# First block of a fused encoder layer: x and V weights fetched and split in parts, seven still matmuls for ten

## The chip, the cores and the metric

The kernel runs on one core of a Trainium2 chip. The core has a matrix engine (TensorE, PE in the profile, with its weight loads as PEld), VectorE (DVE), ScalarE (ACT), GpSimd (POOL) and SyncE (SP). SP, ACT and POOL can issue DMAs; their issues are listed as SPq, ACTq and POOLq. The metric is the device time of one execution in microseconds; less is better.

## The reference

One layer of a hybrid encoder over 512 tokens of width 1024, in float32. Only its opening matters here: a normalised x times a wide input projection.

```python
h = rms_norm(x, g_mix_pre[l])
proj = h @ w_in[l]
q_f, k_f, v_f, f_logit, q_c, k_c, v_c = jnp.split(proj, splits, axis=-1)
```

Columns 1024 to 1535 of `w_in` give the V of the first attention group, and columns 1536 to 1543 its eight forget-gate logits. Two kinds of attention, an output projection, cross-attention into 256 memory tokens and a SwiGLU layer follow.

## The kernel before

x is read transposed, so that its 1024 features lie on the partitions in eight blocks of 128 (`xt`, index k) and its 512 tokens run along the row. The weights come by the same blocks of 128 rows. Every float32 operand is split in two: a high part in a rounded format that the matrix engine takes at its faster rate, and a low part, which is the value less its high part. A product is three matmuls (`mm3`, lines 142 to 146): high by high, high by low, low by high.

The row factor of the RMS norm is applied after the projection, and the gain before it. So x can be multiplied as soon as a block has landed. `x_block` (L293) makes the high part `hTh` of one block on ScalarE (L294) and the low part `hTl` on VectorE (L295). It scales by the gains, which lie in the tile `gn` and come with a DMA on ScalarE's queue (L234).

The first projection is that of V and the gates, 520 columns, cut in `halves` (L279): columns 256 to 519 first (264 wide), then 0 to 255. `load_v` (L246) fetches the 520 columns of a block in one DMA on SyncE's queue (L248) into a tile `raw` with three buffers; `load_x` (L243) fetches x (L244). `v_weights` (L281) makes the high parts `vhi`, for block 0 on VectorE (L285) and for others on ScalarE (L287), and then the low parts `vlo` on VectorE (L289). `v_products` (L307) takes four groups of 128 tokens by two halves by three matmuls, 24 in all, for one block, and adds them up in six accumulators over the eight blocks.

The loads are issued in the order x block 0, V block 0, x block 1, V block 1, x blocks 2 and 3, and so on in pairs (L318 to L328). Beside these, ScalarE squares x in pairs of blocks (`squares`, L301) and VectorE adds the squares (`add_squares`, L305, L338) for the row factor, which a matmul with a column of ones sums up (L255) and a matmul with the identity spreads (L264).

Ahead of the first product the matrix engine runs ten "still" matmuls of a zeroed 128x128 float32 tile with itself (L240, L241), whose result is not used. ScalarE makes one small activation, `warm` (L236), ahead of which its function table is loaded.

The order of the instructions on each engine is fixed when the program is built: a scheduler places them by its own estimate of when their operands are there, with the order of the text as priority. Memsets of later stages (L400, L401), for one, stand on VectorE ahead of block 0.

Of the kernel before, what the change touches and what calls it, by code (L numbers as in the profile page):

```python
# [8 lines left out]
F32 = mybir.dt.float32  # L9
F32R = mybir.dt.float32r  # L10
AF = mybir.ActivationFunctionType
ALU = mybir.AluOpType
AX = mybir.AxisListType

P = 128
SEQ = 512
# [12 lines left out]
G_MIX, G_MEMQ, G_MEMKV, G_FFN, G_FOX, G_CHK, B_F = 0, 8, 16, 24, 32, 36, 40  # L29
# [7 lines left out]
def hybrid_block_kernel(  # L37
# [19 lines left out]
    nc = tc.nc  # L57
    act, dve, pool, pe = nc.scalar, nc.vector, nc.gpsimd, nc.tensor

    cst = ctx.enter_context(tc.tile_pool(name="cst", bufs=1))  # L60
    wp = ctx.enter_context(tc.tile_pool(name="wp", bufs=2))
# [9 lines left out]
    def f32(ap):  # L71
        return ap.bitcast(F32)
# [15 lines left out]
    def gcol(c):  # L88
        return gn[:, c : c + 1]

    def small(n, name):
        serial[0] += 1
        return cst.tile([P, n], F32, tag="small" if n <= NT else "wide", name=f"{name}{serial[0]}", bufs=24 if n <= NT else 4)
# [132 lines left out]
    hTh = big.tile([P, KB, SEQ], F32R, tag="sA", name="hTh")  # L226
    hTl = big.tile([P, KB, SEQ], F32R, tag="sB", name="hTl")
# [3 lines left out]
    with tc.tile_pool(name="mix", bufs=1, reuse_waits="tile") as bp:  # L231
        xt = ox.tile([P, KB, SEQ], F32, tag="x1", name="xt")
        xs = ox.tile([P, KB, SEQ], F32, tag="x2", name="xs")
        nc.scalar.dma_start(gn, gains)  # L234
        warm = small(1, "warm")
        act.activation(warm, ones, AF.Square)  # L236
        acc0 = [bank(tag) for tag in ("s", "s", "a", "o")]
        acc1 = [bank("a"), bank("a")]
        warmed = bank("t")
        for j in range(10):  # L240
            pe.matmul(warmed[:, :P], still, still, start=True, stop=True)  # L241

        def load_x(k, n):  # L243
            nc.sync.dma_start(xt[:, k : k + n, :], x_t[k * P : (k + n) * P, :].rearrange("(k p) n -> p k n", p=P))  # L244

        def load_v(k, n):  # L246
            raw = wp.tile([P, n, 520], F32, tag="raw", name=f"rawv{k}", bufs=3)
            nc.sync.dma_start(raw, w_in[k * P : (k + n) * P, 1024:1544].rearrange("(k p) n -> p k n", p=P))  # L248
            return raw
# [26 lines left out]
        def at_block(parts, k, n=1):  # L276
            each = KB // len(parts)
            return parts[k // each][:, k % each : k % each + n, :]
        halves = (slice(256, 520), slice(0, 256))  # L279

        def v_weights(raw, k, n):  # L281
            for j, cs in enumerate(halves):
                h = at_block(vhi[j], k, n)
# [6 lines left out]
                    out=at_block(vlo[j], k, n), in0=raw[:, :, cs], in1=f32(at_block(vhi[j], k, n)), op=ALU.subtract  # L290
                )

        def x_block(k):  # L293
            act.activation(hTh[:, k, :], xt[:, k, :], AF.Copy, scale=gcol(G_MIX + k))  # L294
            dve.scalar_tensor_tensor(  # L295
                out=hTl[:, k, :], in0=xt[:, k, :], scalar=gcol(G_MIX + k), in1=f32(hTh[:, k, :]),
                op0=ALU.mult, op1=ALU.subtract,
            )

        def squares(k):  # L300
            act.activation(xs[:, k : k + 2, :], xt[:, k : k + 2, :], AF.Square, scale=1.0 / 32.0)  # L301
# [13 lines left out]
                    at_block(vhi[1], k)[:, 0, :], at_block(vlo[1], k)[:, 0, :], k == 0 and t % 2 == 0, k == KB - 1 and t % 2 == 1,  # L315
                )

        load_x(0, 1)  # L318
        raws = {0: load_v(0, 1)}
        load_x(1, 1)  # L320
        raws[1] = load_v(1, 1)
        load_x(2, 2)
# [3 lines left out]
        for k, n in ((0, 1), (1, 1), (2, 2), (4, 2), (6, 2)):  # L326
            if k not in raws:
                raws[k] = load_v(k, n)  # L328
            for j in range(k, k + n):
                x_block(j)  # L330
            v_weights(raws[k], k, n)
            if k:
                squares(k if k > 1 else 0)
            if k in (2, 6):
                add_squares(k - 2, k)
            if k == 6:
                add_squares(0, 4)
                dve.tensor_tensor(out=xs[:, 0, :], in0=xs[:, 0, :], in1=xs[:, 1, :], op=ALU.add)  # L338
            for j in range(k, k + n):
                v_products(j)  # L340
                if j == 6:
                    rcol = feature_rstd(xs, range(1), NT, "rx")
        act.copy(rrow, spread(rcol, NT))

        def v_tile(name):
            return bp.tile([P, NT, 4, 128], F32R, tag="V", name=f"V{name}", bufs=2)

        def raw_v(v, t, a, r):
            a4 = a.rearrange("p (h d) -> p h d", h=4)
            act.activation(v[:, t, :, 0:64], a4, AF.Copy, scale=r)  # L350
            dve.scalar_tensor_tensor(
                out=v[:, t, :, 64:128], in0=a4, scalar=r, in1=f32(v[:, t, :, 0:64]),
                op0=ALU.mult, op1=ALU.subtract,
            )

        z = cst.tile([P, NT, 8], F32, tag="z", name="z")
        first_v = [v_tile("01"), v_tile("00")]
        for t in range(NT):
            r = rcol[:, t : t + 1]
            raw_v(first_v[0], t, acc0[t][:, :256], r)  # L360
            dve.scalar_tensor_tensor(
                out=z[:, t, :], in0=acc0[t][:, 256:264], scalar=r, in1=gn[:, B_F : B_F + 8],
                op0=ALU.mult, op1=ALU.add,
            )
        for t in range(NT):
            raw_v(first_v[1], t, acc1[t // 2][:, (t % 2) * 256 : (t % 2 + 1) * 256], rcol[:, t : t + 1])

        pts = []
        for b in range(2):
# [33 lines left out]

        def group_proj(name):
            q, kt, kl = [], [], []
            if first_v:
                v = first_v.pop(0)
            else:
                v = v_tile(name)
                hi, lo = unit()  # L410
                for t in range(NT):
                    ts = slice(t * P, (t + 1) * P)
                    if t % 2 == 0:
                        acc = bank("a")
                    a = acc[:, (t % 2) * 256 : (t % 2 + 1) * 256]
                    for k in range(KB):
                        mm3(a, hTh[:, k, ts], hTl[:, k, ts], hi[:, k, :], lo[:, k, :], k == 0, k == KB - 1)
                    raw_v(v, t, a, rcol[:, t : t + 1])

            def fin_q(b, acc):  # L420
                t = bp.tile([P, 2, SEQ], F32R, tag="Q", name=f"Q{name}{b}", bufs=3)
                for h, own, other in ((0, H0, H1), (1, H1, H0)):
                    act.activation(t[own, h, :], acc[own, :], AF.Copy, scale=0.125)
                    dve.scalar_tensor_tensor(
                        out=t[other, h, :],
                        in0=acc[own, :],
                        scalar=0.125,
                        in1=f32(t[own, h, :]),
                        op0=ALU.mult,
                        op1=ALU.subtract,  # L430
                    )
                q.append(t)

            def fin_k(b, acc):
                t = bp.tile([P, 2, SEQ], F32R, tag="T", name=f"T{name}{b}", bufs=3)
                l = klz[nkl[0] % len(klz)]
                nkl[0] += 1
                for h, own, other in ((0, H0, H1), (1, H1, H0)):
                    act.copy(t[own, h, :], acc[own, :])
                    dve.tensor_tensor(  # L440
                        out=l[own, h, :], in0=acc[own, :], in1=f32(t[own, h, :]), op=ALU.subtract
                    )
                    act.copy(t[other, h, :], acc[own, :])
                kt.append(t)
                kl.append(l)

            proj_blocks(fin_q)
            proj_blocks(fin_k)
            return q, kt, kl, v
# [158 lines left out]
        for n, (side, g) in enumerate(order):  # L608
            with later(-20):
                q, kt, kl, v = group_proj(f"{side}{g}")  # L610
# [51 lines left out]
    with tc.tile_pool(name="cross", bufs=1, reuse_waits="tile") as cp:  # L662
# [20 lines left out]
        with later(-115):  # L683
            for c in range(4):
                hi, lo = unit()
                acc = bank("a")
                for b in range(2):
                    for k in range(KB):
                        cs = slice(b * P, (b + 1) * P)
# [7 lines left out]
                    out=kT[:, 1, 2 * c : 2 * c + 2, :], in0=a3,  # L697
                    in1=f32(kT[:, 0, 2 * c : 2 * c + 2, :]), op=ALU.subtract,
# [7 lines left out]
        for half in range(2):  # L706
            hi, lo = unit()
            for t in range(NT):
                acc = bank("a")
                for k in range(4):  # L710
                    ts = slice(t * P, (t + 1) * P)
                    mm3(acc, oh[:, 4 + k, ts], ol[:, 4 + k, ts], hi[:, k, :], lo[:, k, :], k == 0, k == 3)
                cs = slice(half * 512, (half + 1) * 512)
                m = mix[:, t, cs]
                dve.scalar_tensor_tensor(
                    out=m, in0=acc, scalar=rs_g[1][:, t : t + 1], in1=m, op0=ALU.mult, op1=ALU.add
# [3 lines left out]
                if half:  # L720
                    r = small(1, "prs")
                    dve.scalar_tensor_tensor(
                        out=r, in0=mix_ms[:, 0, t : t + 1], scalar=EPS, in1=mix_ms[:, 1, t : t + 1],
                        op0=ALU.add, op1=ALU.add,
# [3 lines left out]
                        out=mix[:, t, :], in0=mix[:, t, :], scalar=r, in1=xo[t], op0=ALU.mult, op1=ALU.add  # L728
# [15 lines left out]
        for half in range(2):  # L744
# [12 lines left out]
            cs = slice(half * 512, (half + 1) * 512)  # L757
# [6 lines left out]
        for h in range(4):  # L764
            for o in (oTh, oTl):
                t = quarter("oT").rearrange("p (k n) -> p k n", k=2)
                o += [t[:, 0], t[:, 1]]
        for h in range(4):
            hi, lo = unit()
            q = qq[:, h % 2]  # L770
            for b in range(2):
                acc = bank("a")
                cs = slice(b * P, (b + 1) * P)
                for k in range(KB):
# [3 lines left out]
                    out=q[:, 1, b, :], in0=acc, scalar=1.0 / 16.0, in1=f32(q[:, 0, b, :]),  # L778
                    op0=ALU.mult, op1=ALU.subtract,
                )  # L780
            p = cp.tile([P, NT, NMEM], F32, tag="xp", name=f"xp{h}", bufs=2)
            for i in range(0, NT, 2):
                s = bank("s")
                for j in range(2):
# [8 lines left out]
                    out=nm, in_=s.rearrange("p (j n) -> p j n", j=2), axis=AX.X, op=ALU.max, negate=True  # L793
# [9 lines left out]
                for j in range(2):  # L803
                    dve.tensor_scalar(
                        out=p[:, i + j, :], in0=p[:, i + j, :], scalar1=rs[:, j : j + 1],
# [8 lines left out]
                cs = slice(i * P, (i + 2) * P)  # L814
# [79 lines left out]
        raws, places = [0], []  # L894
# [629 lines left out]
```

## Time and profile before

| | |
|---|---|
| median of 3 runs | 769.16 us (768.88 to 769.38) |
| the profiled execution | 769.24 us |
| its span, first to last instruction | 767.5 us |
| mean granted TensorE clock | 0.997 |
| DMA, bytes moved over the span | 80.05 MB, mean 104 GB/s |
| issues of `xt`, block 0 and 1 | 2, of 256 KB |
| issues of `rawv`, block 0 and 1 | 2, of 260 KB |
| issue of `gn` | 24 KB, 2.9 us to landing |

A row of the timeline gives the start in us from the first instruction, the length in us, the engine, the line of the kernel, the operation, output <- inputs, shapes and a count. In brackets stands the idle time of the engine before it and what ended it. Rows that follow one another on an engine and are alike are merged; their lengths overlap, since engines are pipelined. A float32 still matmul leaves two records. In a table of windows a row holds the window, its length, the busy time of the engine asked for (with its instructions), the granted clock, the DMA engines' busy share and GB/s. In a list of DMA issues the last number is the time from issue to landing.

### The profile page before, as it was taken

What the parts mean: (1) busy time and instruction counts of PE and PEld (TensorE: products, weight loads), DVE (VectorE), ACT (ScalarE), POOL (GpSimd) and SP (SyncE); (2) the same over time, 40 slices, a digit from 0 to 9 for tenths busy, and PEclk for the clock granted to TensorE, in tenths of its full rate; (3) what the DMA queues carried; (4) which work ended last, traced back from release to release, by engine and by line L of the source; (5) the groups of instructions that cost most, each with busy time, mean ns of one, the idle gap of its engine ahead of it and who ended that gap; (6) DMA issues with size and microseconds to landing.
All of it is one profiled execution on the core that took longest, in us unless ns stands there. A gap on an engine that the chain in (4) does not pass through costs nothing.

```text
span 767.5 us, 12862 instructions
## 1 busy us (share of the span) xinstructions
PE 752.7 (98%) x4988; PEld 674.4 (88%) x4988; DVE 595.7 (78%) x1083; ACT 442.9 (58%) x811; POOL 63.6 (8%) x105
## 2 busy tenths in 40 slices
PE   9999999999999999999999999999999999999996
PEld 9977888887778988877778899999999999898985
DVE  8667889789886688555653897999999999987746
ACT  7558889667875457444563635555555557543411
POOL 1001132100321201000001200000000000000001
PEclk9999999999999999999999999999999999999998
DMA  7522123422323735421341132333333323233312
GB/s 268 145 64 76 29 56 95 126 83 60 109 80 83 265 120 186 118 76 59 108 147 48 56 102 65 110 111 110 111 111 110 111 84 110 83 115 107 108 58 109
DMA packets 60748, 80.05 MB, mean 104 GB/s; under 512 B 2704, under 2 KB 43664, under 8 KB 60688
## 3 DMA queue, kind: packets, MB, share of 16 engines
q1 hardware_dynamic: 59264, 74.49, 30.9%
q0 software_dynamic: 1280, 4.72, 1.8%
q8 instruction: 39, 0.64, 0.4%
q14 instruction: 21, 0.17, 0.1%
q10 hardware_dynamic: 144, 0.02, 0.0%
HBM read 77.13 MB, written 2.10 MB: 103 GB/s over the span
## 4 chain that ended last, share of the span: by engine, by line
PE 87%; ACT 6%; DVE 4%; issue 2%; POOL 1%; DMA 1%; DVEq 0%; POOLq 0%; ACTq 0%
PE ps_a L144 13%; PE ps_a L146 13%; PE ps_a L143 13%; PE ps_t L1130 3%; PE ps_t L1127 3%; PE ps_s L1128 3%; PE ps_t L1128 3%; PE ps_s L1127 3%; PE ps_s L1130 3%; PE ps_s L143 2%; PE ps_s L146 2%; PE ps_s L144 2%; PE ps_t L552 2%; PE ps_o L561 2%; PE ps_s L533 1%
## 5 line engine op out<-in xcount | busy, mean ns | idle before, releaser
L126 DVE TENSOR_TENSOR lo<-raw,hi 128x1024 fp32r<-128x1024 f32 x56 | 68.2, 1223 | 20.6 <-ACT hi L125 20.4
L146 PE MATMUL ps_a<-hTh,lo 128*128 128x512 f32 x192 | 76.7, 399 | 0.0
L144 PE MATMUL ps_a<-hTl,hi 128*128 128x512 f32 x192 | 75.9, 395 | 0.0
L143 PE MATMUL ps_a<-hTh,hi 128*128 128x512 f32 x192 | 75.9, 395 | 0.0
L125 ACT CAST hi<-raw 128x1024 fp32r<-128x1024 f32 x56 | 57.8, 1047 | 25.5 <-PE ps_a L144 21.2
L923 DVE TENSOR_TENSOR ring_lo<-sums,ring_hi 128x1024 fp32r<-128x1024 f32 (+1 forms) x39 | 46.7, 1196 | 12.9 <-ACT ring_hi L922 8.5
L922 ACT CAST ring_hi<-sums 128x1024 fp32r<-128x1024 f32 (+1 forms) x39 | 40.1, 1029 | 17.2 <-PE ps_s L1128 15.6
L922 ACT CAST ring_hi<-fraw 128x1024 fp32r<-128x1024 f32 (+1 forms) x26 | 26.7, 1033 | 33.5 <-DVE fraw L1009 13.9
L923 DVE TENSOR_TENSOR ring_lo<-fraw,ring_hi 128x1024 fp32r<-128x1024 f32 (+1 forms) x26 | 31.0, 1201 | 14.2 <-ACT ring_hi L922 14.0
L144 PEld LDWEIGHTS ps_a<-hTl,hi 128*128 128x128 f32 x192 | 36.1, 188 | 6.4
L146 PEld LDWEIGHTS ps_a<-hTh,lo 128*128 128x128 f32 x192 | 36.1, 188 | 6.4
L143 PEld LDWEIGHTS ps_a<-hTh,hi 128*128 128x128 f32 x192 | 36.2, 188 | 5.6
L547 ACT ACTIVATE p<-p,nm 128x128 f32<-128x128 f32 (+1 forms) x64 | 36.1, 565 | 8.1 <-DVE nm L537 7.2
L554 ACT CAST pth<-ps_t 128x128 fp32r<-128x128 f32 (+1 forms) x64 | 27.0, 424 | 14.5 <-PE ps_t L552 13.7
L555 DVE TENSOR_TENSOR ptl<-ps_t,pth 128x128 fp32r<-128x128 f32 (+1 forms) x64 | 30.7, 487 | 5.0 <-ACT pth L554 3.7
L552 PE MATMUL ps_t<-ident,p 128*128 128x128 f32 x160 | 28.2, 275 | 1.1 <-DVE p L549 0.8
L549 DVE TENSOR_SCALAR p<-p,rc 128x128 f32<-128x128 f32 (+1 forms) x64 | 26.8, 418 | 0.1
L552 PEld LDWEIGHTS ps_t<-ident,p 128*128 128x128 f32 x160 | 19.3, 140 | 7.3 <-issue 2.4
L143 PE MATMUL ps_a<-hi,oh 128*128 128x512 f32 x64 | 25.5, 399 | 0.0
L1130 PE MATMUL ps_a<-b,ring_lo 128*128 128x256 f32 (+1 forms) x93 | 25.5, 276 | 0.0
L1127 PE MATMUL ps_a<-b,ring_hi 128*128 128x256 f32 x92 | 25.5, 277 | 0.0
L1128 PE MATMUL ps_a<-b,ring_hi 128*128 128x256 f32 x92 | 25.4, 276 | 0.0
(546 smaller groups left out, 2760.9 us busy)
## 6 DMA issues: line engine op xcount, KB each, us to landing
raw<-in_dram SPq DMA_DIRECT2D x64, 512.0 KB, 3.9
fraw<-in_dram SPq DMA_DIRECT2D x26, 512.0 KB, 3.5
place<-in_dram SPq DMA_DIRECT2D x21, 512.0 KB, 4.3
more_room<-in_dram SPq DMA_DIRECT2D x15, 512.0 KB, 4.3
cb<-in_dram SPq DMA_DIRECT2D x8, 256.0 KB, 2.7
xo<-in_dram POOLq DMA_DIRECT2D x4, 512.0 KB, 7.6
out_dram<-yd SPq DMA_DIRECT2D x8, 256.0 KB, 2.0
rawv<-in_dram SPq DMA_DIRECT2D x3, 520.0 KB, 6.3
```

The source lines that it names most:

```text
L125: act.copy(hi[:, j : j + n, :], raw)
L126: dve.tensor_tensor(out=lo[:, j : j + n, :], in0=raw, in1=f32(hi[:, j : j + n, :]), op=ALU.subtract)
L143: pe.matmul(dst, sh, mh, start=first, stop=False)
L144: pe.matmul(dst, sh, ml, start=False, stop=False)
L146: pe.matmul(dst[:, to], sl, mh[:, to], start=False, stop=last)
L547: act.activation(p[:, :n], p[:, :n], AF.Exp, bias=nm, scale=-1.0, accum_out=sm)
L552: pe.transpose(tp[:, k * P : (k + 1) * P], p[:, k * P : (k + 1) * P], ident)
L922: act.copy(h2, v)
L923: dve.tensor_tensor(out=l2, in0=v, in1=f32(h2), op=ALU.subtract)
L1127: pe.matmul(dst, w[0][:, k, :], b[:, 0, k, :], start=first and k == 0, stop=False, skip_group_check=more)
L1128: pe.matmul(dst, w[0][:, k, :], b[:, 1, k, :], start=False, stop=False, skip_group_check=more)
L1130: pe.matmul(dst[:, to], w[1][:, k, :], b[:, 0, k, to], start=False, stop=last and k == 3, skip_group_check=more,)
```

## The change

Block 0 of x is fetched in two DMAs, tokens 0 to 255 and tokens 256 to 511, both on SyncE's queue. The first is written at the head of the stage, the second where the whole load stood. The V weights of block 0 are fetched in two DMAs by the column halves: columns 256 to 519 on ScalarE's queue behind the gains, columns 0 to 255 on SyncE's queue behind the second half of x. For block 0, `x_block` makes the high part in two activations of 256 tokens and the low part in two VectorE instructions. The still matmuls are seven. A list is renamed from `first_v` to `ready_v`, since `first_v` is now a function; the rename changes nothing else.

```diff
+        raws = {0: wp.tile([P, 1, 520], F32, tag="raw", name="rawv0", bufs=3)}
+        token_halves = (slice(0, 256), slice(256, 512))
+        halves = (slice(256, 520), slice(0, 256))
+
+        def first_x(to):
+            nc.sync.dma_start(xt[:, 0, to], x_t[0:P, to])
+
+        def first_v(queue, cs):
+            queue.dma_start(raws[0][:, 0, cs], w_in[0:P, 1024 + cs.start : 1024 + cs.stop])
+
+        first_x(token_halves[0])
         nc.scalar.dma_start(gn, gains)
+        first_v(nc.scalar, halves[0])
         warm = small(1, "warm")
...
-        for j in range(10):
+        for j in range(7):
             pe.matmul(warmed[:, :P], still, still, start=True, stop=True)
...
-        def x_block(k):
-            act.activation(hTh[:, k, :], xt[:, k, :], AF.Copy, scale=gcol(G_MIX + k))
-            dve.scalar_tensor_tensor(
-                out=hTl[:, k, :], in0=xt[:, k, :], scalar=gcol(G_MIX + k), in1=f32(hTh[:, k, :]),
-                op0=ALU.mult, op1=ALU.subtract,
-            )
+        def x_block(k, parts=(slice(0, SEQ),)):
+            for to in parts:
+                act.activation(hTh[:, k, to], xt[:, k, to], AF.Copy, scale=gcol(G_MIX + k))
+            for to in parts:
+                dve.scalar_tensor_tensor(
+                    out=hTl[:, k, to], in0=xt[:, k, to], scalar=gcol(G_MIX + k), in1=f32(hTh[:, k, to]),
+                    op0=ALU.mult, op1=ALU.subtract,
+                )
...
-        load_x(0, 1)
-        raws = {0: load_v(0, 1)}
+        first_x(token_halves[1])
+        first_v(nc.sync, halves[1])
         load_x(1, 1)
         raws[1] = load_v(1, 1)
...
             for j in range(k, k + n):
-                x_block(j)
+                x_block(j, token_halves if j == 0 else (slice(0, SEQ),))
             v_weights(raws[k], k, n)
```

More of the change, by code (lines that the diff above doesn't have):

```diff
@@ L278, in at_block @@
             return parts[k // each][:, k % each : k % each + n, :]
-        halves = (slice(256, 520), slice(0, 256))
         def v_weights(raw, k, n):
@@ L356, in hybrid_block_kernel @@
         z = cst.tile([P, NT, 8], F32, tag="z", name="z")
-        first_v = [v_tile("01"), v_tile("00")]
+        ready_v = [v_tile("01"), v_tile("00")]
         for t in range(NT):
             r = rcol[:, t : t + 1]
-            raw_v(first_v[0], t, acc0[t][:, :256], r)
+            raw_v(ready_v[0], t, acc0[t][:, :256], r)
             dve.scalar_tensor_tensor(
@@ L365, in hybrid_block_kernel @@
         for t in range(NT):
-            raw_v(first_v[1], t, acc1[t // 2][:, (t % 2) * 256 : (t % 2 + 1) * 256], rcol[:, t : t + 1])
+            raw_v(ready_v[1], t, acc1[t // 2][:, (t % 2) * 256 : (t % 2 + 1) * 256], rcol[:, t : t + 1])
         pts = []
@@ L405, in group_proj @@
             q, kt, kl = [], [], []
-            if first_v:
-                v = first_v.pop(0)
+            if ready_v:
+                v = ready_v.pop(0)
             else:
```

## The prediction

> **What bounds the kernel now.** I read the page first: its head, the busy shares and the chain that ended last.
>
> ```profile
> span 767.5 us, 12862 instructions
> PE 752.7 (98%) x4988; PEld 674.4 (88%) x4988; DVE 595.7 (78%) x1083; ACT 442.9 (58%) x811; POOL 63.6 (8%) x105
> PE 87%; ACT 6%; DVE 4%; issue 2%; POOL 1%; DMA 1%; DVEq 0%; POOLq 0%; ACTq 0%
> ```
>
> TensorE (PE) has work in flight for 752.7 of 767.5 us and holds 87% of the chain. So what the change can win is PE time at the very start, and only as far as PE is not starved later instead. The profiled execution took 769.24 us, 1.74 above its span and 0.08 above the median of the runs shown (769.16).
>
> Next I read the start in order of time, engine by engine (start, length, engine, line, output<-inputs).
>
> ```profile
> 1.05 4.37 PE L241 MATMUL ps_t<-rrow 128*128 128x128 f32 x20 [1.05 <-DVE ones L80]
> 5.55 0.48 PE L143 MATMUL ps_s<-vhi,hTh 128*128 128x264 f32 x2
> ...
> 8.51 0.29 PE L143 MATMUL ps_s<-vhi,hTh 128*128 128x264 f32 x1
> ...
> 6.00:8.00 2.00, 2.00 (x19) 1.00 1.02 383
> ...
> 20.00:30.00 10.00, 10.00 (x86) 1.00 0.59 159
> ```
>
> The still matmuls fill PE to 5.42 (1.05 + 4.37), the first product starts at 5.55, and from 6 to 30 us PE is busy all of every window (the first and the last of five stand here: length, PE busy, clock, DMA share, GB/s). One block of x costs 24 products: 8.51 − 5.55 = 2.96 us, 0.123 each. A first product that starts earlier therefore moves everything behind it, unless operands come too late.
>
> Where do the first operands come from? These are ScalarE (ACT) and VectorE (DVE), with the three ACT instructions ahead of them.
>
> ```profile
> 0.73 0.40 ACTq L234 DMA_DIRECT2D gn<-in_dram  x1
> 1.16 1.28 ACT L236 ACT_TABLE_LOAD   x1 [1.16 <-PEq L1511]
> 2.46 0.20 ACT L236 ACTIVATE warm<-ones 128x1 f32<-128x1 f32 x1
> 3.69 0.72 ACT L294 ACTIVATE hTh<-xt,gn 128x512 fp32r<-128x512 f32 x1 [1.03 <-DMA gn<-in_dram]
> 5.27 0.72 ACT L294 ACTIVATE hTh<-xt,gn 128x512 fp32r<-128x512 f32 x1 [0.86 <-DMA xt<-in_dram]
> 4.44 0.75 DVE L295 SCALAR_TENSOR_TENSOR hTl<-xt,gn,hTh 128x512 fp32r<-128x512 f32 x1 [0.88 <-ACT hTh L294]
> 5.11 0.49 DVE L285 CAST vhi<-rawv 128x264 fp32r<-128x264 f32 x2
> 5.52 0.77 DVE L289 TENSOR_TENSOR vlo<-rawv,vhi 128x264 fp32r<-128x264 f32 x2
> ```
>
> ACT makes x's high part at 3.69, when the gains have landed. DVE then makes the low part, and only behind it, at 5.11, casts the first V weights. That cast ends at 5.40 and the stills at 5.42, so **two things end together** ahead of 5.55: the stills and the cast. Removing one alone wins almost nothing; the change takes up both.
>
> **The change part by part.** Prices of half pieces, from groups by shape in the first 16 us, and landings of the first transfers, one DMA view each:
>
> ```profile
> L289 DVE TENSOR_TENSOR vlo<-rawv,vhi 128x264 fp32r<-128x264 f32 x2 | 0.9, 430 | 0.3 <-ACT vhi L287 0.3
> L289 DVE TENSOR_TENSOR vlo<-rawv,vhi 128x256 fp32r<-128x256 f32 x2 | 0.8, 420 | 0.0
> L285 DVE CAST vhi<-rawv 128x264 fp32r<-128x264 f32 x1 | 0.3, 291 | 0.0
> L287 ACT CAST vhi<-rawv 128x256 fp32r<-128x256 f32 x1 | 0.4, 406 | 0.0
> ...
> xt<-in_dram SPq DMA_DIRECT2D x1, 256.0 KB, 2.7
> gn<-in_dram ACTq DMA_DIRECT2D x1, 24.0 KB, 2.9
> ...
> rawv<-in_dram SPq DMA_DIRECT2D x1, 260.0 KB, 3.2
> 1.18 0.42 SPq L248 DMA_DIRECT2D rawv<-in_dram  x1
> 1.64 0.42 SPq L244 DMA_DIRECT2D xt<-in_dram  x1
> ```
>
> *Stills.* Ten make 20 records, 4.37/20 = 0.219 us each; seven make 14, 3.06 us. PE is free at 1.05 + 3.06 = 4.11.
>
> *x in halves.* The first token half lands no later than the whole block did (0.73 + 2.7 = 3.43). The gains still land at 0.73 + 2.9 = 3.63, so ACT still starts at 3.69. A half has no row; its price lies between 0.36 (half of 0.72) and 0.72, and I take the 0.41 of the 128x256 cast, so the first half is ready at 4.10, the second near 4.5. One more ACT instruction costs nothing on the path: ACT idles 0.86 us ahead of 5.27.
>
> *V weights in halves.* The half that the first products read goes to ACT's queue behind the gains, at about 1.16. Bounds for its landing are the 2.7 and 3.2 us above: 3.86 to 4.36. It has half the bytes of either row, so I take 3.86; the cast of 0.29 then ends at 4.15. Before, 0.15 us passed from that cast's end (5.40) to the product, so **the first product starts at 4.30**, 1.25 us earlier, provided that DVE casts ahead of x's low part.
>
> *Issues.* On ACT the second DMA (0.40) pushes the table load and the warm-up activation from an end of 2.66 to 3.1: still ahead of 3.69, hidden; without that cover it costs 0.4. On SyncE (SP) the x block 0 and V block 0 issues become three; the one at 1.64 for x block 1 slips to about 2.1, and every later load by the same 0.47. Its data lands at 1.64 + 3.6 = 5.24 before. The same bytes stand ahead of it and the engines are full, so I put zero on this. Its bounds are from 0.47 later to 0.3 earlier:
>
> ```profile
> xt<-in_dram SPq DMA_DIRECT2D x1, 256.0 KB, 3.6
> ...
> 2.00:2.25 0.25, 1.00 0.27 92
> 2.25:2.50 0.25, 1.00 0.62 199
> 2.50:2.75 0.25, 1.00 1.11 395
> ```
>
> The earlier end is the idle part of 2.00 to 2.50: 0.25 x 0.73 + 0.25 x 0.38 = 0.28 us that a second queue could fill. [...]
>
> *DVE's block 0 work* gains one instruction. From 4.15 it is two halves of x's low part (0.42 each, as the subtract of that shape), a weight low part (0.43), a cast (0.29) and a low part (0.42): 1.98 us, to 6.1, against 6.29 (5.52 + 0.77). PE meanwhile has four high products and then four with x's low part, so I expect no stall that matters.
>
> *The clock.* Rows at the end of the stills, and the same kind of matmul in the chain at 30 us:
>
> ```profile
> 4.84 0.58 PE L241 MATMUL ps_t<-rrow 128*128 128x128 f32 x3
> 5.04 0.39 PE L241 MATMUL ps_t<-rrow 128*128 128x128 f32 x2
> 5.15 0.28 PE L241 MATMUL ps_t<-rrow 128*128 128x128 f32 x1
> ...
> 29.83 0.89 PE ps_t L264 x8
> ```
>
> At 30 us a record takes 0.111; the stills take 0.219 until about 5.0, where the step falls from 0.20 to 0.11. PE thus ran at half speed to 5.0, although the granted clock reads 1.00. If it changes at 5.0 again, products from 4.30 to 5.0 go at half rate: minus 0.35. At the end of block 0 PE is 1.25 − 0.35 = 0.90 ahead.
>
> *What is late next.* Block 1 hangs on x block 1 (ACT 5.27), and ACT from there runs without a gap; the change moves none of it. So the gain is cut by the slack of later operands:
>
> ```profile
> 9.65 1.14 ACT L287 CAST vhi<-rawv 128x528 fp32r<-128x528 f32 x2
> 9.78 1.22 DVE L305 TENSOR_TENSOR xs<-xs 128x1024 f32<-128x1024 f32 x1
> 10.92 1.30 DVE L289 TENSOR_TENSOR vlo<-rawv,vhi 128x528 fp32r<-128x528 f32 x2
> L289 DVE TENSOR_TENSOR vlo<-rawv,vhi x2: 683/692/702, 10.9 to 11.5; 128x528 fp32r<-128x528 f32 x1, 128x512 fp32r<-128x512 f32 x1
> 12.14 0.28 PE L144 MATMUL ps_s<-vlo,hTh 128*128 128x264 f32 x1
> 15.16 1.30 DVE L289 TENSOR_TENSOR vlo<-rawv,vhi 128x528 fp32r<-128x528 f32 x2
> 17.31 0.28 PE L144 MATMUL ps_s<-vlo,hTh 128*128 128x264 f32 x1
> ```
>
> For blocks 2 and 3 DVE adds squares from 9.78, then makes the weights' low part from 10.92, ready at 11.62 (0.70 for the first). The first product that reads it starts at 12.14: slack 0.52, or 0.37 with the 0.15 that PE took to follow a cast. Blocks 4 and 5 have 17.31 − 15.86 = 1.45. So of 0.90 only 0.37 to 0.52 survives; I take 0.45. **Sum:** 769.24 − 0.45 = 768.79, or 768.7 against the median. The bounds of what can survive are none and the whole 1.25.
>
> **The rivals.** *DVE keeps its order* (x's low part, then the cast). From 4.13 two halves of 0.42 and the cast of 0.29 end at 5.26, the product starts near 5.4: 0.15 won, 769.0. For it: before stands in this order. Against: the half of V should land before x's high part is done, so the cast is ready first.
>
> *The supply moves too.* Two queues bring x block 1 up to 0.28 earlier and DVE's low part is placed ahead of the squares: 0.9 to 1.25 won, 768.1. For it: DVE's adding is not needed until much later. Against: ACT's cast at 9.65 still ends its first half near 10.2 (9.65 + 0.57).
>
> *The clock stays low*, the case on the slower side. Seven stills end at 4.11; if the pause before the products makes PE's busy time count anew, the 3.95 us that it took from 1.05 to 5.0 run from 4.30 to 8.25, at half rate. PE has then done 1.98 us of products, where before it had done 2.70: 0.72 later, nothing downstream gives it back, 769.9; were the first product as late as 5.4, it is 3.95/2 − 0.15 = 1.8 late, 771.0. It decides by whether the steps halve near 5.0 or later. For it: the present stills reach past the change, seven don't. Against: the pause is some 0.2 us only. [...]
>
> *It doesn't do what it says:* the half on ACT's queue lands no earlier than V did (1.18 + 3.2 = 4.38), and nothing moves: 769.2.
>
> **How the numbers follow.** Forecast 0.44; DVE's order 0.17; supply moves 0.17; clock 0.14; nothing 0.08. What a measurement of this kernel can tell from no change is about 0.2%, 1.54 us: 767.6 to 770.7. No mechanism reaches 767.6 by itself; later instructions may be placed anew behind the shift, for which I leave 0.06. Slower than 770.7 needs the low clock and a late start: 0.05. That leaves 0.89 for the same. The range, 767.8 to 770.1, goes from the whole 1.25 (767.9) to the clock's case (769.9) with the 0.2 by which a run lies from the median.
>
> **What would show it.** First product near 4.3, the 0.219 steps ending near 5.0, block 1 beginning near 7.6, and a PE pause before the first product on block 2's low weights, which should still come at 11.6 to 11.8. Wrong if the cast stands behind both low parts of x, if half-rate products last beyond 5.5, or if products of block 2 run on before 11.5.

## The result

The changed kernel takes 780.59 us (median, 779.83 to 780.83, 4 runs) against 769.27 of the kernel before beside it: a ratio of 1.0141, 95% interval 1.0129 to 1.0154. It is 11.3 us slower, where 0.45 us faster was forecast, with a range that ended at 770.1. The profiled execution took 780.46 us, 11.2 more than that of before.

The head of the page after, with busy shares and the chain that ended last:

```profile
span 778.7 us, 12855 instructions
PE 764.4 (98%) x4982; PEld 683.5 (88%) x4982; DVE 596.6 (77%) x1084; ACT 443.4 (57%) x812; POOL 63.6 (8%) x105
...
PE 86%; ACT 6%; DVE 4%; issue 2%; DMA 1%; POOL 1%; SPq 0%; DVEq 0%; POOLq 0%; ACTq 0%
```

PE is busy for 11.7 us more (764.4 against 752.7), with no more instructions recorded. It is not waiting longer for others; it takes longer for the same work. DVE, ACT and POOL are within 1 us of before.

The opening explains little of it. PE, ACT and DVE rows of the changed kernel, in order of time:

```profile
1.05 3.36 PE L253 MATMUL ps_t<-rrow 128*128 128x128 f32 x14 [1.05 <-DVE ones L80]
4.51 0.78 PE L143 MATMUL ps_s<-vhi,hTh 128*128 128x264 f32 x2
...
6.39 0.42 PE L144 MATMUL ps_s<-vlo,hTh 128*128 128x264 f32 x1
6.61 0.42 PE L146 MATMUL ps_s<-vhi,hTl 128*128 128x264 f32 x1
6.83 0.37 PE L144 MATMUL ps_a<-vlo,hTh 128*128 128x264 f32 x1
7.03 0.29 PE L146 MATMUL ps_a<-vhi,hTl 128*128 128x264 f32 x1
7.16 0.28 PE L144 MATMUL ps_o<-vlo,hTh 128*128 128x264 f32 x1
...
8.59 0.29 PE L143 MATMUL ps_s<-vhi,hTh 128*128 128x264 f32 x1
...
13.17 0.39 PE L144 MATMUL ps_s<-vlo,hTh 128*128 128x264 f32 x1 [0.33 <-DVE vlo L299]
6.47 0.72 ACT L305 ACTIVATE hTh<-xt,gn 128x512 fp32r<-128x512 f32 x1 [2.16 <-DMA xt<-in_dram]
4.06 0.30 DVE L295 CAST vhi<-rawv 128x264 fp32r<-128x264 f32 x1 [0.50 <-DMA rawv<-in_dram]
```

The first product comes at 4.51, 1.04 us earlier than before. Its steps are 0.22 us until about 7.0 and 0.12 from there, so the clock rose some 2 us later than in the profile of before: the trace's record of the clock begins the full share at 7.00 us here and at 5.01 there. ScalarE could begin x block 1 at 6.47 instead of 5.27. Block 1 begins at 8.59 against 8.51, and the first product on block 2's low weights comes at 13.17 against 12.14. So the opening loses 1.03 us by then, and about 10 us are lost later.

They are lost in long streams of matmuls that wait for nothing. One window in the feed-forward stage, whose matmuls are called gate products below, for the kernel before and then for the changed one (window, its length, PE busy and instructions, clock, DMA share, GB/s):

```profile
480.00:630.00 150.00, 150.00 (x1325) 1.00 0.35 110
```

```profile
480.00:630.00 150.00, 150.00 (x1285) 1.00 0.34 106
```

PE is busy all of it and the granted clock is 1.00 in both. Yet the same 150 us hold 1325 matmuls before and 1285 after: 113.2 against 116.7 ns each. Groups of these matmuls by shape, from the same window of the changed kernel, then of the one before (the number before the last bar is the mean length in ns):

```profile
L1140 PE MATMUL ps_s<-tlo,ring_hi 128*128 128x256 f32 x64 | 18.1, 282 | 0.0
...
L1142 PE MATMUL ps_a<-b,ring_lo 128*128 128x256 f32 x63 | 17.4, 277 | 0.0
```

```profile
L1130 PE MATMUL ps_a<-b,ring_lo 128*128 128x256 f32 x64 | 17.7, 276 | 0.0
...
L1128 PE MATMUL ps_s<-tlo,ring_hi 128*128 128x256 f32 x63 | 17.4, 276 | 0.0
```

All groups of the two windows taken together, products of `tlo` and `thi` take 5 to 6 ns more than before, those of `b` beside them at most 3. These tiles lie in buffers named `hi` and `lo`, and the change moved those. In the changed kernel `raws[0]` is created at the head of the stage, ahead of `vhi` and `vlo`. In both builds the buffers of the pool lie in the order in which they are first asked for, so the three `raw` buffers now lie in front. The built programs give these addresses in bytes within a partition, two or three buffers of a name:

```
          before                  changed                 start within 256 bytes
hi        6656, 15104             19136, 27584            0 -> 192
lo        23552, 32000            36032, 44480            0 -> 192
raw       40448, 44608, 48768     6656, 10816, 14976      unchanged
hTh       53248                   53248                   unchanged
```

The two `hi` and two `lo` buffers moved by 3 x 4160 = 12480 bytes, which is 48 x 256 + 192, and no buffer of another pool moved. **Theory A:** the start of these buffers within 256 bytes sets the pace of the matmuls that read them. **Rival B:** the halves, or work placed anew behind them, cost the time. **Rival C:** the seven stills and the clock do.

### The profile page after: what moved, and what is told of

Same layout as the page of the kernel before. It is cut to its first block, busy times and chain, and to the rows that moved or that the text cites. A ratio compares the mean times of both kernels' runs of the same rounds, so it can differ in the third digit from the quotient of the medians.

```text
span 778.7 us, 12855 instructions
## 1 busy us (share of the span) xinstructions
PE 764.4 (98%) x4982; PEld 683.5 (88%) x4982; DVE 596.6 (77%) x1084; ACT 443.4 (57%) x812; POOL 63.6 (8%) x105
## 4 chain that ended last, share of the span: by engine, by line
PE 86%; ACT 6%; DVE 4%; issue 2%; DMA 1%; POOL 1%; SPq 0%; DVEq 0%; POOLq 0%; ACTq 0%
PE ps_a L144 13%; PE ps_a L146 13%; PE ps_a L143 13%; PE ps_t L1139 3%; PE ps_t L1142 3%; PE ps_s L1142 3%; PE ps_t L1140 3%; PE ps_s L1140 3%; PE ps_s L1139 3%; PE ps_s L144 2%; PE ps_s L143 2%; PE ps_s L146 2%; PE ps_t L564 2%; PE ps_o L573 2%; PE ps_s L545 1%
## 5 line engine op out<-in xcount | busy, mean ns | idle before, releaser
L146 PE MATMUL ps_a<-hTh,lo 128*128 128x512 f32 x192 | 77.2, 402 | 0.0
L143 PE MATMUL ps_a<-hTh,hi 128*128 128x512 f32 x192 | 76.1, 397 | 0.0
L146 PEld LDWEIGHTS ps_a<-hTh,lo 128*128 128x128 f32 x192 | 36.2, 189 | 6.3
L143 PEld LDWEIGHTS ps_a<-hTh,hi 128*128 128x128 f32 x192 | 36.2, 189 | 5.9
L143 PE MATMUL ps_a<-hi,oh 128*128 128x512 f32 x64 | 25.7, 401 | 0.0
L144 PE MATMUL ps_a<-lo,oh 128*128 128x512 f32 x64 | 25.6, 400 | 0.0
L146 PE MATMUL ps_a<-hi,ol 128*128 128x512 f32 x64 | 25.5, 399 | 0.0
```

The lines of the kernel that those rows point to most:

```text
L143: pe.matmul(dst, sh, mh, start=first, stop=False)
L144: pe.matmul(dst, sh, ml, start=False, stop=False)
L146: pe.matmul(dst[:, to], sl, mh[:, to], start=False, stop=last)
```

## The experiments

### Buffers back, and buffers alone

The first kernel is the change with the two tiles created in the old order.

```diff
+        vhi, vlo = (...)
         raws = {0: wp.tile([P, 1, 520], F32, tag="raw", name="rawv0", bufs=3)}
...
-        vhi, vlo = (...)
```

> The changed kernel, with one edit: the tiles vhi and vlo are created ahead of the tile raws[0], as in the kernel before, so that the hi and lo buffers stand again 12480 bytes lower, at multiples of 256 bytes. Loads, halves and seven stills stay. Theory A (the buffers' place sets the pace of the matmuls): the 256-wide step of the gate products goes from 119 back to 113 ns, and the time comes back to 768 to 771 us, where the opening alone (clock, first loads) decides the rest. Rival B (the halves, or loads that are placed anew behind them, cost the time): about 780 us as in the changed kernel. Rival C (the seven stills and the clock): also about 780.

770.30 us against 769.73, ratio 1.0011 (1.0002 to 1.0019). Ten of the eleven microseconds are gone, with every load, half and still of the change in place. The same window of this kernel:

```profile
480.00:630.00 150.00, 150.00 (x1325) 1.00 0.34 110
```

The second is the converse: the kernel before, in which only that tile is created first.

```diff
+        raws = {0: wp.tile([P, 1, 520], F32, tag="raw", name="rawv0", bufs=3)}
         nc.scalar.dma_start(gn, gains)
...
-        raws = {0: load_v(0, 1)}
+        nc.sync.dma_start(raws[0], w_in[0:P, 1024:1544].rearrange("(k p) n -> p k n", p=P))
```

> The kernel before, with one edit: the tile raws[0] is created at the head of the stage, ahead of vhi and vlo; its load is one DMA at its old place, x in one load, ten stills. Only buffers move: hi and lo by 12480 bytes up, raw to the front. Theory A: 10 to 11 us slower than before, 779 to 780.5, with 119 ns steps in the gate products. Rivals B and C: no change, 769.2.

780.03 us against 769.73, ratio 1.0136 (1.0123 to 1.0149):

```profile
480.00:630.00 150.00, 150.00 (x1285) 1.00 0.34 106
```

The loss is there whole, with 1285 matmuls in the window as in the changed kernel, and without a half, an extra DMA or a still less. Theory A holds; B and C as the cause of the eleven microseconds fall.

### How the place counts

Three kernels keep `raw` in front and push `hi` and `lo` on by 64, 128 or 192 bytes. The filler tile of the next pool, `pad_big`, is cut by as much, so that nothing else moves.

```diff
+        wp.tile([P, 16], F32, tag="shift", name="shift", bufs=1)
...
-    big.tile([P, 80], F32, tag="pad", name="pad_big")
+    big.tile([P, 64], F32, tag="pad", name="pad_big")
```

> The kernel with raws[0] created first (nothing else of the change), and an unused tile of 64 bytes ahead of hi and lo, with the filler tile of the next pool cut by the same 64 bytes so that nothing behind moves. hi and lo now lie 12544 bytes above their old place, but on a multiple of 256 again. Theory A1 (the start within 256 bytes sets the pace): back to the time of before, 769 to 770.3, gate steps of 113 ns. Rival A2 (the distance, or which side of raw they lie on): 780 as without the filler.

> As the kernel before this one, with a filler of 128 bytes: hi and lo start 64 bytes past a multiple of 256. Theory A1, any start off a multiple of 256 slows the moving operand: 776 to 781, 119 ns steps in the gate products. Rival A3 (only moving and stationary operands that share their place modulo 128 bytes collide): gate products, whose stationary operand lies 64 past, slow down alike; the 512-wide products with stationary hi stay near 227 ns or gain.

> The same with a filler of 192 bytes: hi and lo start 128 past a multiple of 256. Theory A1: 776 to 781, 119 ns steps. Rival A3 (only the place modulo 128 counts): back to before, 769 to 770.3, 113 ns steps.

The window of the three, with starts at 0, 64 and 128 within 256 bytes:

```profile
480.00:630.00 150.00, 150.00 (x1325) 1.00 0.34 110
```

```profile
480.00:630.00 150.00, 150.00 (x1279) 1.00 0.33 106
```

```profile
480.00:630.00 150.00, 150.00 (x1294) 1.00 0.33 104
```

A filler of 64 bytes brings the time back to that of before: 769.57 us, ratio 0.9997 (0.9988 to 1.0006). With a start at 64 it is 780.59 (1.0137, 1.0120 to 1.0154), at 128 it is 776.92 (1.0093, 1.0078 to 1.0108). So the distance and the order of the buffers do not matter (A2 falls), and the place modulo 128 alone does not decide (A3 falls, since 128 is still 7.2 us slower and, as the table below shows, 512-wide steps with the stationary operand in `hi` or `lo` slow down too). A1's 776 to 781 holds for both.

The traces give the step from the start of one matmul to the start of the next. The trace names the operands of a matmul in the order moving, stationary; the stationary one is loaded as weights ahead of the matmul, in a row of its own (LDWEIGHTS): before, the weights of the matmul at 480.26 us load from 480.15, where the matmul ahead of it starts. A plain float32 matmul of 128 columns leaves two records of 0.111 us each in the profile of before (L264, 30 us), 256 columns in the rounded format one every 0.12 (L143 to L146, 29 us). I paired the matmuls of each trace with the addresses of their operands in the built program and took the median step in ns between two matmuls of the same width; the stationary address is that of the following matmul, whose weights load meanwhile, as at 480.15. All places are in bytes past a multiple of 256. Some operands lie 64 or 192 bytes into their buffer, so that their place is not that of the buffer's start. In brackets stands the number of steps where it matters.

```
start of hi and lo within 256 bytes:              0            64           128          192
256 wide: moving in hi/lo, stationary at 64       113          120 (911)    118 (911)    119 (911)
256 wide: moving elsewhere at 0, stationary 64    113          114 (1198)   113 (1198)   114 (1198)
256 wide: moving elsewhere at 0, stationary
  in hi/lo at 64, 128, 192, 0                     113          119 (355)    117 (355)    120 (355)
256 wide: moving in hi/lo at 192, 0, 64, 128,
  stationary at 0                                 117          120 (178)    118 (178)    119 (178)
512 wide: moving at 0, stationary in hi/lo        227          233 (501)    232 (501)    230 (501)
512 wide: moving in hi/lo, stationary at 0        227          233 (357)    232 (357)    233 (357)
512 wide: neither in hi/lo, both at 0             227          227 (437)    227 (437)    227 (437)
```

The two rows whose operands do not lie in `hi` or `lo` stay within 1 ns in every kernel. In the first row and in that of 512 columns, a moving operand off the multiple of 256 costs 5 to 7 ns a matmul. A1 speaks of the moving operand alone, and that is too narrow: another place of the stationary operand costs 4 to 7 ns at 256 columns (113 to 117, 119 or 120) and 3 to 6 at 512 (227 to 230, 232 or 233), and beside a stationary operand at 0 a 256-wide step takes 117 to 120 in all four places of the moving one. At 192, the case of the change, the sum of medians is 911 x 6 + 357 x 6 + 501 x 3 + 355 x 7 = 11.6 us, beside the 10.3 measured (780.03 − 769.73). Taken step by step between the profiles instead of by medians, these four groups add up to 9.4 us at 192, 10.4 at 64 and 7.8 at 128, where the profiled executions lie 11.2, 11.9 and 7.8 us above that of before (780.39, 781.10 and 777.00 against 769.24). So the operands' places carry most of the loss in each of three kernels that lose different amounts. What in the chip makes these nanoseconds the runs do not show.

### The stills and the clock

> The kernel before with seven stills for ten and nothing else. Theory A: within 1 us of before, 768.8 to 770.3: the first product still waits for the cast that ends near 5.4 us, and the clock may rise later than at 5.0. Rival C (the seven stills cost the 11 us through the clock): near 780.

```diff
-        for j in range(10):
+        for j in range(7):
```

771.14 us against 769.73, ratio 1.0017 (1.0009 to 1.0026): slower by 1.3 us by the ratio, beyond the 770.3 that was expected at most. PE in that kernel:

```profile
5.43 0.78 PE L143 MATMUL ps_s<-vhi,hTh 128*128 128x264 f32 x2 [1.03 <-DVE vhi L285]
...
8.20 0.42 PE L146 MATMUL ps_o<-vhi,hTl 128*128 128x264 f32 x1
8.42 0.37 PE L144 MATMUL ps_a<-vlo,hTh 128*128 128x256 f32 x1
8.63 0.28 PE L146 MATMUL ps_a<-vhi,hTl 128*128 128x256 f32 x1
8.74 0.28 PE L143 MATMUL ps_a<-vhi,hTh 128*128 128x256 f32 x1
```

PE pauses for 1.03 us behind the stills, and the products then go in steps of 0.22 until 8.6, where they halve to 0.12. From 5.43 to 8.60 at half rate costs 3.17 / 2 = 1.6 us in this profile, about what the execution took more than that of before (770.91 against 769.24). That is the low clock of the prediction's rival.

That the missing stills made the clock late is not shown, however. Ten stills do not secure an early rise. The kernel before with `raws[0]` created first, which has ten stills, starts its products at half rate too:

```profile
6.24 0.42 PE L143 MATMUL ps_a<-vhi,hTh 128*128 128x264 f32 x1
6.46 0.36 PE L143 MATMUL ps_o<-vhi,hTh 128*128 128x264 f32 x1
6.65 0.28 PE L143 MATMUL ps_a<-vhi,hTh 128*128 128x256 f32 x1
6.77 0.28 PE L144 MATMUL ps_s<-vlo,hTh 128*128 128x264 f32 x1
```

Their steps are 0.22, 0.19 and 0.12, a rise near 6.6. In the nine profiles with ten stills the trace's record of the clock puts the rise at 4.0, 4.3, 5.0, 5.7, 5.8, 5.9, 6.6, 7.1 and 7.2 us; in the three with seven, at 4.2 (buffers back), 7.0 (the changed kernel) and 8.6. So the late rise in the changed kernel can't be put down to its seven stills, and these profiles do not tell what sets the moment. Measured is the time: seven stills alone cost 1.3 us over 11 runs.

### What the halves are worth

The next kernel has the halves, the buffers in the old order and ten stills; it ran in two batches.

```diff
-        for j in range(7):
+        for j in range(10):
```

> The first of these kernels (buffers back in place, halves) with ten stills. If the clock is what the stills are for, it lies 0 to 1 us below the one with seven; if the stills only delay the first product, 0 to 1 us above it. Theory A: 768 to 770.5 either way. Rival B: near 780.

> The kernel with halves, buffers back in place and ten stills once more, for a profile with a full clock. If halves bring the first product forward but x block 1 still lands near 6.5 us, block 1 begins near 8.6 as with seven stills and the spread of the row factor near 30; if x block 1 lands near 5.2, block 1 begins before 8.2 and the spread stands at 29.3 or earlier. Time 769.5 to 771.

The ratios are 1.0020 (1.0003 to 1.0037) and 1.0006 (0.9997 to 1.0016); one run of the first batch, 778.69 us at a granted clock of 0.946, lifts its ratio and widens its interval (the other eleven average 770.5). With the 1.0011 of seven stills, the intervals overlap: within the halves, seven and ten stills can't be told apart, and neither beats the kernel before. Rows of the second batch's profile:

```profile
4.83 0.49 PE L143 MATMUL ps_s<-vhi,hTh 128*128 128x264 f32 x2
5.16 0.28 PE L143 MATMUL ps_a<-vhi,hTh 128*128 128x264 f32 x1
5.77 0.39 PE L144 MATMUL ps_s<-vlo,hTh 128*128 128x264 f32 x1 [0.33 <-DVE vlo L299]
...
8.40 0.29 PE L143 MATMUL ps_s<-vhi,hTh 128*128 128x264 f32 x1
...
12.61 0.39 PE L144 MATMUL ps_s<-vlo,hTh 128*128 128x264 f32 x1 [0.33 <-DVE vlo L299]
5.72 0.72 ACT L305 ACTIVATE hTh<-xt,gn 128x512 fp32r<-128x512 f32 x1 [1.41 <-DMA xt<-in_dram]
8.39 1.34 ACT L305 ACTIVATE hTh<-xt,gn 128x512 fp32r<-128x512 f32 x2 [0.39 <-DMA xt<-in_dram]
4.89 0.47 DVE L307 SCALAR_TENSOR_TENSOR hTl<-xt,gn,hTh 128x256 fp32r<-128x256 f32 x1
5.29 0.76 DVE L299 TENSOR_TENSOR vlo<-rawv,vhi 128x264 fp32r<-128x264 f32 x2
```

The first product is 0.72 us earlier than before (4.83), but within block 0 PE stands 0.33 us for the weights' low part, which DVE makes behind both low parts of x. So block 1 begins only 0.11 earlier (8.40 against 8.51). x block 1 comes at 5.72 (before 5.27) and block 2 at 8.39 (before 7.46), and the first product on block 2's low weights comes at 12.61, behind another wait and 0.47 later than before. The spread of the row factor comes at 30.26 (before 29.67), as the expectation had it for late data. Two more kernels ask whether the extra loads on SyncE made the blocks late. One has x in one load and both V halves on ACT's queue, the other x in one load and the V halves on two queues; both have ten stills and the old buffers.

```diff
-        first_x(token_halves[0])
+        first_x(slice(0, SEQ))
         nc.scalar.dma_start(gn, gains)
         first_v(nc.scalar, halves[0])
+        first_v(nc.scalar, halves[1])
...
-        first_x(token_halves[1])
-        first_v(nc.sync, halves[1])
```

(The second kernel lacks the line that is added for `halves[1]` on ScalarE's queue and keeps the last line; `x_block` takes block 0 whole in both.)

> Buffers in place, ten stills, x block 0 in one load and both V halves on ACT's queue behind the gains, so that SyncE issues x block 1 at about 1.2 us instead of 2.1. Theory D (the extra loads ahead of x block 1 on SyncE make it and the blocks behind it late, and that ate what the halves won): x block 1's high part starts near 5.2 instead of 5.7 to 6.6, the first product comes between 4.7 and 5.4, and the time is that of before or up to 0.5 us below it, 769.2 to 769.8 beside a before of 769.7. Rival E (the data comes as the memory gives it, whatever the order of issue): x block 1 as late as with the halves, 770 to 770.6.

> Buffers in place, ten stills, x block 0 in one load, V block 0 in halves, one on ACT's queue and one on SyncE's: x block 1 is issued at 1.64 as before. Theory D: between the kernel with all halves (1.0006 to 1.002 times before) and before: 769.5 to 770.1, x block 1's high part at 5.2 to 5.7. Rival E: as with all halves.

The first took 771.40 us against 769.59, ratio 1.0023 (1.0014 to 1.0032); the second 770.00, ratio 1.0004 (0.9995 to 1.0013). The first kernel's rows for x block 1, V's second half and PE by windows:

```profile
4.69 0.72 ACT L306 ACTIVATE hTh<-xt,gn 128x512 fp32r<-128x512 f32 x1 [0.18 <-DMA xt<-in_dram]
7.68 0.29 DVE L296 CAST vhi<-rawv 128x256 fp32r<-128x256 f32 x1 [2.04 <-DMA rawv<-in_dram]
...
7.20:9.10 1.90, 0.00 (x0) 1.00 1.05 401
9.10:10.60 1.50, 1.45 (x12) 1.00 1.05 407
10.60:14.00 3.40, 3.40 (x19) 0.51 0.96 356
```

x block 1, issued at 1.18, was indeed early: 4.69, ahead of every other profile here, as theory D has it and rival E has not. But V's second half on ACT's queue came at 7.68, DVE's next work stood behind it, and PE was without a product from 7.2 to 9.1. From 10.6 the clock was at half for 3.4 us. The gain that D expected did not come. In the second kernel x block 1 came at 5.91, although issued at 1.63, which D doesn't explain. Of the profiles with a whole x load that is issued near 1.64, five had it between 5.17 and 5.52, two at 5.91 and 6.18; with halves of x, four had 5.06, 5.72, 6.47 and 6.61. The spread within each kind is as large as the difference, so whether the halves themselves delay x block 1 stays open.

What the halves do to the loads as a whole is plainer. From 1 to 8 us the DMA engines moved 285 to 301 GB/s in the six profiles with block 0 of x and V whole, 273 and 283 in the two with V alone in halves, and 246 to 265 in the four with both in halves. The packets tell why this may be so: from 1 to 6 us, before and in the changed kernel,

```profile
DMA packets 848, 1.34 MB, mean 269 GB/s; under 512 B 208, under 2 KB 208, under 8 KB 848
```

```profile
DMA packets 1039, 1.16 MB, mean 232 GB/s; under 512 B 233, under 2 KB 745, under 8 KB 1039
```

in the changed kernel 512 of 1039 packets are half rows of 1024 or 1056 bytes; a whole row is a packet of 2048 or 2080, and before all but 208 of 848 are that. So 745 packets are under 2 KB instead of 208. No run varies the packets alone, so that they are the cause is argued and not shown.

## Why the prediction was wrong

**The step that failed** is the inventory of parts. The prediction priced the stills, the DMAs, the halves, the clock and the slack behind them, and let all else stand: "No mechanism reaches 767.6 by itself; later instructions may be placed anew behind the shift, for which I leave 0.06. Slower than 770.7 needs the low clock and a late start: 0.05." A line of the diff that issues nothing, the creation of `raws[0]` ahead of `vhi` and `vlo`, got no price. It costs 10.3 us by itself and stands in no rival: the prediction took for granted that a matmul behind the opening takes as long as before ("A first product that starts earlier therefore moves everything behind it, unless operands come too late"), and 256-wide steps went from 113 to 119 and 120 ns instead. The text of the kernel held the warning: load units take their place in `hi` and `lo` with offsets `AS_WEIGHTS, AS_MOVING = 16, 48` (64 and 192 bytes), and `pad_big` is a tile that nobody reads. Someone had to place operands by bytes.

**What the prediction priced**, the opening, went like this:

- *First product at 4.30:* it came at 4.51 in the changed kernel and at 4.59 in the one with the buffers back. DVE did cast ahead of x's low part, as the provision asked, and the rival with the old order did not come. The half of V came a little later than priced (the cast began at 4.06, not 3.86).
- *Clock at 5.0, minus 0.35:* it rose at about 7.0 in the changed kernel. From 4.51 to there at half rate costs 2.5 / 2 = 1.25 us, which by itself takes the whole lead of 1.04. The rival with the low clock named this loss. Its prices were 0.72, and 1.8 for a first product as late as 5.4; with seven stills alone the product came at 5.43, and 1.3 us were lost. Its reason, that the pause behind fewer stills makes PE's busy time count anew, no run shows: with the buffers back and the same seven stills the rise came at 4.2, ahead of the first product at 4.59, and with ten stills it came anywhere from 4.0 to 7.2.
- *No stall by DVE's block 0 work:* with the halves and a clock that rose ahead of the first product there was one. With the buffers back PE waits 0.24 us for DVE's `vlo` at 5.84, with ten stills 0.33 at 5.77. A half of x's low part took 0.48 us, where 0.42 was priced.
- *x block 1 unmoved, zero for the later issues:* it came 1.20 late (6.47 against 5.27), more than the bound of 0.47 allowed. The reason given for the zero, the same bytes ahead of it and full engines, does not hold: with halves the engines carried less (232 against 269 GB/s from 1 to 6 us). In the changed kernel that did not set the start of block 1, since PE was busy with block 0 to 8.59, up to about 7.0 at the low clock. With the buffers back it did: x block 1 came at 6.61, ScalarE's cast of block 1's weights stood behind it, and PE waited.

```profile
4.59 0.48 PE L143 MATMUL ps_s<-vhi,hTh 128*128 128x264 f32 x2 [0.20 <-ACT hTh L305]
5.84 0.39 PE L144 MATMUL ps_s<-vlo,hTh 128*128 128x264 f32 x1 [0.24 <-DVE vlo L299]
8.64 0.39 PE L143 MATMUL ps_s<-vhi,hTh 128*128 128x264 f32 x1 [0.39 <-ACT vhi L297]
```

- *Block 2's low weights as the cap:* PE did pause there (0.33 us for DVE's `vlo`), at 13.17 instead of 11.6 to 11.8, since x blocks 1 and 2 were late (6.47 and 8.96, before 5.27 and 7.46).
- *The forecast of −0.45 for the opening:* with the buffers back the change measures 1.0011 times before, +0.6 us from the medians. It gives no gain in any of the variants tried. So the opening's terms failed too, by about 1 us of the 11.8 between forecast and result.

No version here is faster than the kernel before. Three can't be told from it: that with the 64-byte filler (0.9997), which has none of the change's loads, the halves with ten stills in their second batch (1.0006), and the V halves alone (1.0004).

## What to carry to other kernels

Moving the line that creates a buffer can move the buffers behind it, here `hi` and `lo` by 12480 bytes; compare the addresses of the two builds before pricing the instructions, here modulo 256 bytes for what the matrix engine reads (113 ns or 117 to 120 for a 256-wide step by that place). When a kernel becomes slower while PE is busy all the time, count matmuls in one window of both traces: 1325 against 1285 in 150 us named the loss where no wait did. An earlier start won here only what the next operands allowed (a first product 0.72 us earlier, block 1 0.11), and the split loads moved the same bytes in smaller packets, from 1 to 6 us at 232 GB/s against 269. And the moment at which the clock rises has to be read over several profiles before it is put down to an edit: here it lay between 4.0 and 7.2 us with the same ten warm-up matmuls.

## What the hardware showed that I had not expected

- A 256-wide matmul step was 113 ns with the moving operand at a multiple of 256 bytes and the stationary one 64 past, and 118 to 120 in the other places tried for the moving operand beside the same stationary one; a 512-wide step was 227 with both at a multiple and 230 to 233 with one off it. Over the kernel this is 0.9 to 1.4%.
- For 256 columns the stationary operand did best 64 bytes past (113, against 117 to 120 elsewhere, with the moving one at 0), while for 512 the best place seen was 0 (227 against 233 at 64). One rule does not serve both.
- In one profile PE had no product for 1.9 us, and from 1.5 us behind that the granted clock was at half for 3.4 us, which the window from 10.60 to 14.00 shows as 0.51. Ahead of the first rise the profile prints 1.00 while the steps are twice as long (0.22 us against 0.12), so there the steps have to be read.
